# Softmax weights left undivided through the value product, divided afterwards by reciprocals that return from DRAM as rows

## The chip, the cores and the metric

One core of a Trainium2 chip runs one launch of a hybrid decoder layer. The metric is device time of the launch in microseconds (us); lower is better. Engines: TensorE (PE; its weight loads are shown apart, as PEld), VectorE (DVE), ScalarE (ACT), GpSimd (POOL) and SyncE (SP), which issues nearly all DMAs here.

## The reference, cut to what matters

One layer, 512 tokens, 2048 channels. Two of its three token mixers are attentions over heads of 64:

```python
# A: 8 heads, mixture of three dilated causal patterns, combined by their softmax denominators
# C: 16 query heads, 2 kv heads, causal window 128, a learned sink per head
p = jnp.exp(s - m[..., None])
denom = jnp.sum(p, axis=-1)
denom = denom + jnp.exp(sk - m)          # C only: the sink
o = jnp.einsum('nbhgqk,nbkhd->nbqhgd', p, vb)
o = o / denom_t[..., None]
...
x = x + mix @ w_out[l]
```

So the division by the softmax sum comes after the product with v in the reference; it may as well be made on the weights before it. Around the mixers stand the input projection (2048 to 3840 columns), a convolution mixer (B), the output projection, and a SwiGLU block with 5632 hidden channels, all in float32.

## The kernel before

**Stages.** The input projection runs as 30 tiles of 128 columns (PROJ gives their order: cv, ck, then the c queries between b's u and gate tiles, then the a tiles), each 48 matmuls of 128x512: every factor is split in a high and a low part and three products are summed. The output projection follows in two halves, first over eight c row tiles and then over the rest (ROWS), then the up and down products, which take from about 500 us to the end. The change touches only mixers a and c.

**What sets the order.** Every engine runs its instructions in the order in which the program writes them. The program is written along TensorE's projections: `ticks` counts steps of two k tiles (6 matmuls; in the output half later 12), and `ticks.after(n, fn)` puts a piece of a mixer n steps on. C_TICKS and A_TICKS give the distances between a mixer's pieces. Weights come through seven raw buffers, loaded by `pump` (L243, on SP) as soon as the split that read a buffer is done; `split_up_to` makes the high part on ACT (L289, wh) and the low part on DVE (L263, wl), two units ahead of TensorE. 73 slots of 128x512 hold all else.

**A mixer** (`attention`, L795 on, names c0 to c7 and a0 to a3) is a pair of heads; its two halves `head(0)` and `head(1)` fill the two halves of the partitions of one row tile `mix`. Of each head: `scores` (L814, L815, PE), masks and row maxima on DVE, exponentials on ACT (L835 for c, with their sums; L889 for a), then the division on DVE: for c the sink is added, the reciprocal of the four sums of a token is taken (L842), and one product scales all 128x512 weights (L844). For a each of three blocks is multiplied by the mask's counts with its sums (L896), its reciprocal taken (L898), and its one or two row tiles are scaled (L900). PE turns the weights (L850, L916, tiles c1t, a0t and so on), they are split in high (ACT) and low (DVE, c1lp, a0pl), for c sorted to blocks on POOL (L870 and L873, tiles c1ph, c1pl), and `weigh` multiplies them with v (L940 and L941, tiles c1o, a1o). `out_high` (L949, ACT) and `out_rows` (L954, DVE) add the two parts into `mix`. `split_mix` makes mh and ml of a row tile for the output projection (L994, L995), and `residual` (L1073) adds a product to xr.

**Trips through DRAM.** The sums of squares of a q or k tile leave at L642 and come back turned at L647; the scales of a k tile leave at L708 and come back as rows, each broadcast over 64 partitions, at L714, for `scale` on DVE (L723).

Of the kernel before, what the change touches and what calls it, by code (L numbers as in the profile page):

```python
# [9 lines left out]
F32 = mybir.dt.float32  # L10
# [4 lines left out]
ALU = mybir.AluOpType  # L15

P = 128
T = 512
NT = T // P
D = 2048  # L20
KT = D // P
HD = 64
HALF = (slice(0, HD), slice(HD, 2 * HD))
# [93 lines left out]
def kernel(ctx: ExitStack, tc: tile.TileContext, xT, wi, wo, wgu, wd, cst_in, outT):  # L117
    nc = tc.nc
    cp = ctx.enter_context(tc.tile_pool(name="consts", bufs=1))
# [16 lines left out]
    ticks = Ticks()  # L136

    def slot(name, dt=F32, cols=T):
        return sp.tile([P, cols], dt, name=name, tag="s")
# [11 lines left out]
    sums = defaultdict(list)  # L151
# [23 lines left out]
    def up_block(pair, m, half, j):  # L175
# [4 lines left out]
    bufs = {"A": dict(zip(("21", "11", "s", "22"), ("21a", "22a", "sa", "22b"))),  # L180
            "B": dict(zip(("21", "11", "s", "22"), ("21b", "11", "12", "sb")))}

    for n in range(2 * NBLOCKS):
# [15 lines left out]
        bufs = {c: {"21": b["22"], "11": b["21"], "s": b["s"], "22": b["11"]} for c, b in bufs.items()}  # L199
# [6 lines left out]
    for t, (g, r) in enumerate(DOWN):  # L206
# [7 lines left out]
        for k in ("21A", "11A", "21B", "11B", "22A", "22B", "12A", "12B"):  # L214
            c = k[2]
# [14 lines left out]
        bufs = {c: {"21": b["22"], "11": b["21"], "s": b["s"], "22": b["11"]} for c, b in bufs.items()}  # L230
# [255 lines left out]
    for k in range(KT):  # L486
# [9 lines left out]
        elif k < 4 or k % 2 == 0:  # L496
            wh, wl = next_unit()
            o = 0
# [294 lines left out]
    def attention(kind, box, mix, mi, heads):  # L793
# [3 lines left out]
            fl, we = fl + 2, we + 3  # L797
        name = mi
        us = UNITS[kind]
        st = {}  # L800

        def head(h):
            es = {}
            d = cp.tile([P, 4, NT], F32, name=f"{name}d{h}", tag="soft", bufs=6)
            mx, nm, den, rd = (d[:, i] for i in range(4))
            banks = {}

# [32 lines left out]
            def packed_norm():  # L840
                nc.vector.tensor_add(den, den, mx)
                nc.vector.reciprocal(rd, den)  # L842
                by = es["e"].rearrange("p (i c) -> p i c", c=P)
                nc.vector.tensor_mul(by, by, rd[:, :, None].to_broadcast([P, NT, P]))  # L844

            def packed_flip():
                b = bank(f"{name}t{h}")
# [43 lines left out]

            def norm(u):
                e = es[u]
                s = slice(us[u][0][0], us[u][-1][0] + 1)
                for i, k0, n, o in us[u]:
                    nc.vector.scalar_tensor_tensor(e[:, o:o + n], e[:, o:o + n], 1.0, mult_a[:, T - n:],  # L896
                                                   op0=ALU.mult, op1=ALU.mult, accum_out=den[:, i:i + 1])
                nc.vector.reciprocal(rd[:, s], den[:, s])  # L898
                for i, k0, n, o in us[u]:
                    nc.vector.tensor_scalar(e[:, o:o + n], e[:, o:o + n], rd[:, i:i + 1], None, op0=ALU.mult)  # L900

            ph, pl = {}, {}

# [42 lines left out]
            def out_high(b):  # L946
                if h == 0:
                    st["mix"] = slot(f"mix_{mi}")
                nc.scalar.copy(st["mix"][HALF[h]], b[HALF[1 - h]])  # L949
                ticks.after(EV, out_rows, b)  # L950

            def out_rows(b):
                m = st["mix"]
                nc.vector.tensor_add(m[HALF[h]], m[HALF[h]], b[HALF[h]])  # L954
                if h == 1:
                    mix[mi] = m
                    if late:
                        ticks.after(1, split_mix, mi)

            at_v = (len(us) - 1) * step + s1 + sx + s2 + fl + len(TBANKS[kind]) - 1 + ev + EV + we  # L960
            t0 = max(ticks.now + ready, head_at[0], box["q at"] - s1, box["k at"], box["v at"] - at_v)
            head_at[0] = t0 + every
            t0 -= ticks.now
            for u in range(len(us)):
                tu = t0 + u * step
                ticks.after(tu, scores, u)
                if kind == "c":
                    ticks.after(tu + s1, pack, u)
                    continue
                ticks.after(tu + s1, top, u)  # L970
                ticks.after(tu + s1 + sx, exps, u)
                ticks.after(tu + s1 + sx + s2, norm, u)
            tu = t0 + (len(us) - 1) * step + s1 + sx
            if kind == "c":
                ticks.after(tu, packed_exps)
                ticks.after(tu + s2, packed_norm)
                ticks.after(tu + s2 + fl, packed_flip)
            else:
                for t in range(len(TBANKS[kind])):
                    ticks.after(tu + s2 + fl + t, flip, t)  # L980
            ticks.after(t0 + at_v, weigh)

        head(0)
        head(1)


    mix, late = {}, []
# [34 lines left out]
    for name in PROJ[HEAD4:]:  # L1022
        kind, what, j = name[0], name[1], name[2:]
        if name == PROJ[-2]:
            for n, row in enumerate(ROWS[:8]):
                ticks.after(6 + n, split_mix, row)
        b = project(name)
        if kind == "b":
            ticks.after(0, glu_u if what == "u" else glu, int(j), b)
            continue  # L1030
        if kind == "c":
            box = Heads(shared) if j else shared
        else:
            box = boxes.setdefault(j, {})
        if what == "k":
            do_k(box, b, name, 1 if kind == "c" else 0)
        elif what == "v":
            do_v(box, b, name)
        else:
            do_q(box, b, name)  # L1040
        if what == "q":
            if kind == "a":
                boxes.pop(j)
            attention(kind, box, mix, kind + j, (int(j), int(j) + 8) if kind == "c" else None)
# [85 lines left out]
    for half in range(2):  # L1130
        for i, n in enumerate(OUT_ORDER[half]):
# [4 lines left out]
            for kk in range(8):  # L1136
# [4 lines left out]
                s = slice(kk * P, (kk + 1) * P)  # L1141
# [552 lines left out]
```

## Time and profile before

| | us |
|---|---|
| timed runs, median of 3 (lowest, highest) | 1843.22 (1843.0, 1843.69) |
| the profiled execution's own time | 1845.39 |
| its span, first instruction to last | 1843.6 |
| PE busy | 1835.2 |
| DVE busy | 1445.8 |
| ACT busy | 1312.1 |
| POOL busy | 1026.2 |
| TensorE's granted clock | 1.00 of full speed |

Times in a row of the profile count from the span's start. "Idle before, releaser" in a row, and the view of waits, tell what ended an engine's idle time. A window's row gives the busy time of each engine in a stretch and the count of its instructions. Matmuls are pipelined, and their ends in the trace are modelled.

### The profile page before, as it was taken

The page shows a single profiled execution, that of the slowest core. Times are in us where ns is not written, and L with a number is a line of the kernel's source. Part 1 is how long each engine was busy: PE and PEld are TensorE (multiplying, and loading weights), DVE is VectorE, ACT ScalarE, POOL GpSimd, SP SyncE. Part 2 cuts the span into 40 slices and gives each one's busy share as a digit, 9 for nine tenths or more (in the row PEclk, how much of TensorE's full clock was granted, in tenths as well). Part 3 has the DMA queues.
Part 4 walks back from the last instruction along what each step waited for, and adds up shares of the span by engine and source line. Part 5 has one row for each costly group of instructions (what it writes and reads, how often), then busy time and mean ns, then how long its engine had stood idle before and what let it go on. Part 6 is the DMA issues. An engine that isn't in the chain of part 4 may idle for free.

```text
span 1843.6 us, 26502 instructions
## 1 busy us (share of the span) xinstructions
PE 1835.2 (100%) x8314; PEld 1522.4 (83%) x8314; DVE 1445.8 (78%) x2063; ACT 1312.1 (71%) x1784; POOL 1026.2 (56%) x790
## 2 busy tenths in 40 slices
PE   9999999999999999999999999999999999999998
PEld 7888888888888888888888888888888888888887
DVE  6789988997689877778777787777777777777777
ACT  6345554553458788888888888888887778777775
POOL 0126644110003557886788767878676558776552
PEclk9999999999999999999999999999999999999999
DMA  7353345353343457677867778677687679877735
GB/s 276 87 150 93 87 121 153 107 161 116 124 149 103 115 151 191 188 213 182 225 187 200 201 188 226 181 209 199 182 273 258 204 225 295 257 254 260 240 119 110
DMA packets 398924, 334.61 MB, mean 181 GB/s; under 512 B 184256, under 2 KB 326720, under 8 KB 398784
## 3 DMA queue, kind: packets, MB, share of 16 engines
q1 hardware_dynamic: 398208, 332.14, 62.3%
q8 instruction: 66, 1.08, 0.3%
q10 hardware_dynamic: 576, 0.79, 0.1%
q14 instruction: 74, 0.61, 0.1%
HBM read 258.46 MB, written 65.98 MB: 176 GB/s over the span
## 4 chain that ended last, share of the span: by engine, by line
PE 95%; DVE 3%; DMA 1%; issue 0%; ACT 0%; SPq 0%; POOL 0%; DVEq 0%; POOLq 0%; ACTq 0%
PE out L1281 15%; PE out L1279 15%; PE out L1282 15%; PE out L1544 7%; PE out L1546 7%; PE out L1545 7%; PE o L322 3%; PE o L323 3%; PE o L324 3%; PE cq L322 2%; PE cq L324 2%; PE cq L323 2%; PE in L324 1%; PE in L323 1%; PE in L322 1%; PE aq L322 1%
## 5 line engine op out<-in xcount | busy, mean ns | idle before, releaser
L1279 PE MATMUL out<-wh,h 128*128 128x512 f32 x1232 | 479.2, 389 | 0.0
L1281 PE MATMUL out<-wl,h 128*128 128x512 f32 x1232 | 479.2, 389 | 0.0
L1282 PE MATMUL out<-wh,h 128*128 128x512 f32 x1232 | 479.2, 389 | 0.0
L1279 PEld LDWEIGHTS out<-wh,h 128*128 128x128 f32 x1232 | 231.2, 188 | 48.1
L1282 PEld LDWEIGHTS out<-wh,h 128*128 128x128 f32 x1232 | 231.2, 188 | 48.0
L1281 PEld LDWEIGHTS out<-wl,h 128*128 128x128 f32 x1232 | 231.2, 188 | 47.9
L1545 PE MATMUL out<-wl,a 128*128 128x512 f32 x620 | 240.4, 388 | 0.1
L1544 PE MATMUL out<-wh,a 128*128 128x512 f32 x620 | 240.4, 388 | 0.0
L1546 PE MATMUL out<-wh,a 128*128 128x512 f32 x620 | 240.3, 388 | 0.0
L289 ACT CAST wh<-w 128x1024 fp32r<-128x1024 f32 (+2 forms) x94 | 96.9, 1031 | 121.6 <-PE o L323 48.0
L1554 DVE TENSOR_TENSOR y<-y,out 128x512 f32<-128x512 f32 x192 | 128.5, 684 | 47.8 <-PE out L1546 46.1
L263 DVE TENSOR_TENSOR wl<-w,wh 128x1024 fp32r<-128x1024 f32 (+2 forms) x95 | 115.0, 1211 | 30.9 <-ACT wh L289 27.9
L1545 PEld LDWEIGHTS out<-wl,a 128*128 128x128 f32 x620 | 116.4, 188 | 24.5 <-DVE wl L285 0.5
L1546 PEld LDWEIGHTS out<-wh,a 128*128 128x128 f32 x620 | 116.4, 188 | 23.8
L1544 PEld LDWEIGHTS out<-wh,a 128*128 128x128 f32 x620 | 116.4, 188 | 23.8
L573 DVE SCALAR_TENSOR_TENSOR y<-bu,cst,y 128x511 f32<-128x511 f32 (+14 forms) x120 | 92.0, 767 | 1.3
L322 PE MATMUL o<-mh_c,wh 128*128 128x512 f32 x128 | 51.1, 399 | 0.2 <-DVE xr L1073 0.2
L322 PE MATMUL cq<-hh,wh 128*128 128x512 f32 x128 | 50.3, 393 | 0.0
L324 PE MATMUL o<-mh_c,wl 128*128 128x512 f32 x128 | 50.0, 391 | 0.0
L323 PE MATMUL o<-ml_c,wh 128*128 128x512 f32 x128 | 50.0, 390 | 0.0
L323 PE MATMUL cq<-hl,wh 128*128 128x512 f32 x128 | 49.9, 390 | 0.0
L324 PE MATMUL cq<-hh,wl 128*128 128x512 f32 x128 | 49.9, 390 | 0.0
(2351 smaller groups left out, 4766.5 us busy)
## 6 DMA issues: line engine op xcount, KB each, us to landing
od<-a SPq DMA_DIRECT2D x154, 256.0 KB
a<-od SPq DMA_DIRECT2D x154, 256.0 KB
w<-in_wi SPq DMA_DIRECT2D x58, 512.0 KB
w<-in_wo SPq DMA_DIRECT2D x32, 512.0 KB
x<-in_xT SPq DMA_DIRECT2D x16, 256.0 KB
xr<-in_xT SPq DMA_DIRECT2D x16, 256.0 KB
x2d<-xr SPq DMA_DIRECT2D x16, 256.0 KB
z<-x2d SPq DMA_DIRECT2D x64, 64.0 KB
```

What stands on the lines that cost most here:

```text
L263: fn(*args)
L289: (nc.vector.tensor_copy if u == 0 else nc.scalar.copy)(hi[:, :n], t[:, :n])
L322: nc.tensor.matmul(out, wh, xh, start=start, stop=False)
L323: nc.tensor.matmul(out, wh, xl, start=False, stop=False)
L324: nc.tensor.matmul(out, wl, xh, start=False, stop=stop)
L1279: nc.tensor.matmul(b, x[:, high], wh[:, s], start=c == f == 0 and q in (7, 1, 5, 2), stop=False, skip_group_check=True)
L1281: nc.tensor.matmul(b, x[:, high], wl[:, s], start=False, stop=False, skip_group_check=True)
L1282: nc.tensor.matmul(b, x[:, low], wh[:, s], start=False, stop=c == f == 1, skip_group_check=True)
L1544: nc.tensor.matmul(b[:, lo:hi], x[:, high], wh[:, s], start=start, stop=False, skip_group_check=True)
L1545: nc.tensor.matmul(b[:, lo:hi], x[:, high], wl[:, s], start=False, stop=False, skip_group_check=True)
L1546: nc.tensor.matmul(b[:, lo:hi], x[:, low], wh[:, s], start=False, stop=last, skip_group_check=True)
L1554: getattr(eng, op)(t, t, src)
```

## The change

The division moves behind the product with v. The weights e are turned and multiplied as they come from the exponentials (c) or from the masks' counts (a). The reciprocals rd of a head's 512 sums (128 partitions by 4) are written to a DRAM tile `sums`, one word at a time, so that they stand there as a row of 512 (`sums_leave`). Two steps ahead of the second head's product with v, both rows are read back, each broadcast over the 64 partitions of its half (`sums_back`, a new slot `by`). One step after the second half of `mix` is added, one product on DVE multiplies the whole row tile by `by` (`scale_out`), and what followed there (`mix[mi] = m`, `split_mix`) comes after it. For a, one reciprocal is taken of all four columns after the last block, in place of three. The pool of the small tiles d grows from 6 to 8.

```diff
-        st = {}
+        st = {"sums": tc.dram_tile([2, T], F32, name=f"{name}sums")}
+
+        def sums_leave(h, rd):
+            nc.sync.dma_start(st["sums"][h].rearrange("(i p) -> p i", p=P), rd)
+
+        def sums_back():
+            st["by"] = slot(f"{name}by")
+            for h in range(2):
+                nc.sync.dma_start(st["by"][HALF[h]], st["sums"][h:h + 1].to_broadcast([HD, T]))
+
+        def scale_out():
+            m = st["mix"]
+            nc.vector.tensor_mul(m, m, st.pop("by"))
+            mix[mi] = m
+            if late:
+                ticks.after(1, split_mix, mi)
...
-            d = cp.tile([P, 4, NT], F32, name=f"{name}d{h}", tag="soft", bufs=6)
+            d = cp.tile([P, 4, NT], F32, name=f"{name}d{h}", tag="soft", bufs=8)
...
                 nc.vector.reciprocal(rd, den)
-                by = es["e"].rearrange("p (i c) -> p i c", c=P)
-                nc.vector.tensor_mul(by, by, rd[:, :, None].to_broadcast([P, NT, P]))
+                ticks.after(1, sums_leave, h, rd)
...
-                nc.vector.reciprocal(rd[:, s], den[:, s])
-                for i, k0, n, o in us[u]:
-                    nc.vector.tensor_scalar(e[:, o:o + n], e[:, o:o + n], rd[:, i:i + 1], None, op0=ALU.mult)
+                if u == len(us) - 1:
+                    nc.vector.reciprocal(rd, den)
+                    ticks.after(1, sums_leave, h, rd)
...
                 if h == 1:
-                    mix[mi] = m
-                    if late:
-                        ticks.after(1, split_mix, mi)
+                    ticks.after(1, scale_out)
...
             ticks.after(t0 + at_v, weigh)
+            if h == 1:
+                ticks.after(t0 + at_v - 2, sums_back)
```

The order of PE and of POOL is the same in both kernels; ACT's differs in one or two places by a row. Three places on DVE and SP follow (out<-in by the program's names with buffer numbers; the changed kernel's lines are 13 to 15 higher).

DVE at about 173 to 178 us of the profile before, in the second head of c1, ahead of the gate tile bg that ACT and POOL wait for. Before:

```order
L573 SCALAR_TENSOR_TENSOR y_1218<-bu_708,cst,y_1218 128x491
L841 TENSOR_TENSOR c1d_1131<-c1d_1131 128x4
L842 RECIPROCAL c1d_1131<-c1d_1131 128x4
L844 TENSOR_TENSOR c1e_1701<-c1e_1701,c1d_1131 128x512
L562 TENSOR_TENSOR bg_1765<-bg_1585,r1b 128x512
L263 TENSOR_TENSOR wl_1742<-w_1288,wh_1741 128x1024
```

Now:

```order
L573 SCALAR_TENSOR_TENSOR y_1221<-bu_708,cst,y_1221 128x491
L856 TENSOR_TENSOR c1d_1134<-c1d_1134 128x4
L857 RECIPROCAL c1d_1134<-c1d_1134 128x4
L562 TENSOR_TENSOR bg_1776<-bg_1594,r1b 128x512
L263 TENSOR_TENSOR wl_1754<-w_1291,wh_1753 128x1024
```

The scaling of the weights between the reciprocal and bg is gone.

SP at about 150 to 177 us before, with the loads of raw weights (w) and the trip of cq2. Before:

```order
L243 DMA w_1602<-in_wi 128x1024
L642 DMA cq2d<-cq2p 32x4x4 x4
L685 DMA cq_1580<-cq2l 64x512
L686 DMA cq_1581<-cq2l 64x512
L243 DMA w_1697<-in_wi 128x1024
L647 DMA cq2t<-cq2d 128x16
L243 DMA w_1775<-in_wi 128x1024
L243 DMA w_1843<-in_wi 128x1024
```

Now:

```order
L243 DMA w_1611<-in_wi 128x1024
L803 DMA c1sums<-c1d_1133 128x4x1
L642 DMA cq2d<-cq2p 32x4x4 x4
L685 DMA cq_1588<-cq2l 64x512
L686 DMA cq_1589<-cq2l 64x512
L243 DMA w_1706<-in_wi 128x1024
L647 DMA cq2t<-cq2d 128x16
L808 DMA c3by<-c3sums 64x512 x2
L243 DMA w_1786<-in_wi 128x1024
L803 DMA c1sums<-c1d_1134 128x4x1
L243 DMA w_1856<-in_wi 128x1024
```

A write of c1's first sums comes ahead of the trip of cq2, the two reads of c3's rows behind it, and a write of c1's second sums between two loads.

DVE at about 396 to 403 us before, at the start of the output projection, where a1's row tile is finished and the residual xr of an output tile follows. Before:

```order
L954 TENSOR_TENSOR mix_a_4081<-mix_a_4081,a1o_4199 64x512
L995 TENSOR_TENSOR ml_a_4268<-mix_a_4081,mh_a_4267 128x512
L263 TENSOR_TENSOR wl_4191<-w_3735,wh_4190 128x1024
L896 SCALAR_TENSOR_TENSOR a2e_4253,a2d_3860<-a2e_4253,mult_a 128x512
L898 RECIPROCAL a2d_3860<-a2d_3860 128x1
L900 TENSOR_SCALAR a2e_4253<-a2e_4253,a2d_3860 128x512
L880 ISA a2s_4255,a2d_3861<-a2s_4255,bias_a 128x256
L880 ISA a2d_3861 128x1
L880 ISA a2s_4255,a2d_3861<-a2s_4255,bias_a 128x128
L880 ISA a2d_3861 128x1
L883 SCALAR_TENSOR_TENSOR a2d_3861<-a2d_3861,aq2r 128x2
L1073 TENSOR_TENSOR xr_4183<-xr_4183,o_0_4187 128x512
```

Now:

```order
L967 TENSOR_TENSOR mix_a_4108<-mix_a_4108,a1o_4230 64x512
L812 TENSOR_TENSOR mix_a_4108<-mix_a_4108,a1by 128x512
L263 TENSOR_TENSOR wl_4222<-w_3764,wh_4221 128x1024
L909 SCALAR_TENSOR_TENSOR a2e_4279,a2d_3891<-a2e_4279,mult_a 128x512
L912 RECIPROCAL a2d_3891<-a2d_3891 128x4
L894 ISA a2s_4281,a2d_3892<-a2s_4281,bias_a 128x256
L894 ISA a2d_3892 128x1
L894 ISA a2s_4281,a2d_3892<-a2s_4281,bias_a 128x128
L894 ISA a2d_3892 128x1
L897 SCALAR_TENSOR_TENSOR a2d_3892<-a2d_3892,aq2r 128x2
L1008 TENSOR_TENSOR ml_a_4315<-mix_a_4108,mh_a_4314 128x512
L1086 TENSOR_TENSOR xr_4214<-xr_4214,o_0_4218 128x512
```

The product with the rows (a1by) stands where the low part ml_a stood; ml_a now comes right ahead of xr, and the scaling of a2's last block is gone.

More of the change, by code (lines that the diff above doesn't have):

```diff
@@ L893, in norm @@
                 e = es[u]
-                s = slice(us[u][0][0], us[u][-1][0] + 1)
                 for i, k0, n, o in us[u]:
```

## Prediction

> **What bounds the kernel now.** I read the page first: the span, the busy shares and the shares of the chain that ended last.
>
> ```profile
> span 1843.6 us, 26502 instructions
> PE 1835.2 (100%) x8314; PEld 1522.4 (83%) x8314; DVE 1445.8 (78%) x2063; ACT 1312.1 (71%) x1784; POOL 1026.2 (56%) x790
> ...
> PE 95%; DVE 3%; DMA 1%; issue 0%; ACT 0%; SPq 0%; POOL 0%; DVEq 0%; POOLq 0%; ACTq 0%
> ```
>
> PE is idle for 1843.6 - 1835.2 = 8.4 us in all. The change lies in the projections and the first half of the output product, about 110 to 500 us, so I cut that stretch into windows (columns: PE, PEld, DVE, ACT, POOL busy, each with its count, then clock, DMA share, GB/s), with one quiet window from the later stage beside it.
>
> ```profile
> 175.00:200.00 25.00, 24.19 (x125) 20.20 (x124) 24.09 (x46) 13.90 (x32) 16.61 (x24) 1.00 0.26 75
> 325.00:350.00 25.00, 24.72 (x129) 20.80 (x128) 23.34 (x62) 11.45 (x19) 5.06 (x11) 1.00 0.32 84
> 350.00:375.00 25.00, 24.83 (x123) 20.53 (x121) 24.35 (x68) 12.34 (x22) 2.67 (x2) 1.00 0.34 94
> 650.00:675.00 25.00, 25.00 (x112) 20.70 (x111) 20.09 (x24) 21.11 (x24) 19.57 (x10) 1.00 0.62 171
> ```
>
> The reader should see two things. DVE is nearly full here (24.1 and 24.4 of 25 us), and still PE loses only a few tenths per window: 0.81, 0.28 and 0.17 us. So taking work from DVE pays only where PE visibly waits. Those places are the next view, the waits of PE between 100 and 500 us (total, times, longest), and under it those of its weight loads.
>
> ```profile
> PE c1o L941 <- POOL c1pl L873: 0.8, 2, 0.5
> PE a0t L916 <- DVE a0e L900: 0.3, 1, 0.3
> PE o L322 <- DVE xr L1073: 0.2, 1, 0.2
> PE a1t L916 <- DVE a1e L900: 0.2, 1, 0.2
> ```
>
> ```profile
> PEld c1o L941 <- POOL c1pl L873: 1.3, 2, 0.8
> ...
> PEld o L322 <- ACT a2e L889: 0.6, 1, 0.6
> PEld a0t L916 <- DVE a0e L900: 0.5, 1, 0.5
> PEld a1t L916 <- DVE a1e L900: 0.4, 1, 0.4
> ```
>
> Four places, 0.8 + 0.3 + 0.2 + 0.2 = 1.5 us by PE's rows and 1.3 + 0.6 + 0.5 + 0.4 = 2.8 us by the loads'. Matmul ends are modelled, so a gap may be partly hidden under the matmul drawn before it, and I take the loss to lie between. That is all that this stage has to give.
>
> The weight loads' 83% is weighed against that. The quiet window has 20.70 of 25 us, also 83%, at 112 matmuls and with PE busy throughout, so 83% is what a stretch without waits looks like here. The Trainium skill (Perfetto Trace Analysis, section "Identifying the Most-Contended Engine") says to judge TensorE's headroom by the share of LDWEIGHTS and by the useful arithmetic, not by matmul busy time; by that rule 17% is free and DVE could be the bound. The quiet window speaks against it; its time is rival 3.
>
> **The change part by part: DVE.** These rows are the operations taken out, with the ns of one (c kind; two of the four groups of the a kind; its reciprocals).
>
> ```profile
> L844 DVE TENSOR_TENSOR c1e<-c1e,c1d x2: 691/692/692, 164.2 to 174.2; 128x512 f32<-128x512 f32 x2
> ```
>
> ```profile
> L900 DVE TENSOR_SCALAR a0e<-a0e,a0d 128x128 f32<-128x128 f32 (+3 forms) x8 | 3.0, 392 | 0.2
> ...
> L900 DVE TENSOR_SCALAR a2e<-a2e,a2d 128x128 f32<-128x128 f32 (+3 forms) x8 | 2.9, 384 | 0.2
> ```
>
> ```profile
> L898 DVE RECIPROCAL a0d<-a0d x6: 164/164/167, 320.4 to 345.3; 128x1 f32<-128x1 f32 x4, 128x2 f32<-128x2 f32 x2
> ```
>
> The eight c mixers lose 16 x 0.692 = 11.1 us; the four a mixers lose 3.0 + 3 x 2.9 = 11.7 us of scalings and, with 24 reciprocals becoming 8, 16 x 0.164 = 2.6 us. Added are 12 products of a row tile with its reciprocals, 128x512 with two inputs in SBUF. That is the form of L844, so 0.692 each; the bounds are the a kind's longest scaling, 0.485, below, and about double a L844 above. 12 x 0.692 = 8.3 us. DVE sheds 11.1 + 11.7 + 2.6 - 8.3 = 17.1 us (8.8 to 19.6 with those bounds for the product).
>
> What lies on the path is only what ends PE's four waits. The first one hangs on a chain through three engines:
>
> ```profile
> 174.21 0.69 DVE L844 TENSOR_TENSOR c1e<-c1e,c1d 128x512 f32<-128x512 f32 x1
> 174.82 0.68 DVE L562 TENSOR_TENSOR bg<-bg,r1b 128x512 f32<-128x512 f32 x1
> ...
> 175.54 0.63 ACT L563 ACTIVATE bg<-bg 128x512 f32<-128x512 f32 x1 [2.01 <-DVE bg L562]
> ...
> 176.25 1.53 POOL L564 TENSOR_TENSOR bu<-bu,bg 128x512 f32<-128x512 f32 x1 [3.41 <-ACT bg L563]
> ```
>
> ACT waited 2.01 us for DVE's bg, POOL 3.41 us for ACT, and POOL's queue behind it (the powers of cq2, then the selections of c1's weights) ends in the wait of c1o. DVE runs back to back here (no idle in brackets), and in the new order the scaling ahead of bg is gone, here and in the row above that began at 164.2, so bg comes at least 2 x 0.69 = 1.4 us sooner (c3's product is queued only after it). POOL moves up with it, by more than the longest single wait of 0.8 us: both waits of c1o should go. The waits of a0t and a1t are for the last scaling of a weight block; that scaling is gone, and the turn needs only the mask product, a reciprocal (0.16) and a scaling (0.485) earlier: both go. The fourth is in this view, DVE, and last the matmul that waited:
>
> ```profile
> 396.52 0.69 DVE L954 TENSOR_TENSOR mix_a<-mix_a,a1o 64x512 f32<-64x512 f32 x1 [0.47 <-ACT mix_a L949]
> 397.90 0.69 DVE L995 TENSOR_TENSOR ml_a<-mix_a,mh_a 128x512 fp32r<-128x512 f32 x1 [0.69 <-ACT mh_a L994]
> ...
> 400.57 0.48 DVE L900 TENSOR_SCALAR a2e<-a2e,a2d 128x512 f32<-128x512 f32 x1
> ...
> 402.21 0.69 DVE L1073 TENSOR_TENSOR xr<-xr,o 128x512 f32<-128x512 f32 x1
> ...
> 403.05 0.47 PE L322 MATMUL o<-mh_c,wh 128*128 128x512 f32 x1 [0.20 <-DVE xr L1073]
> ```
>
> Here a1's product comes in (+0.69), the idle 0.69 before ml_a goes because ml_a is queued later, and the scaling goes (-0.48): xr ends about 0.5 us sooner, and the wait goes too. Of 1.5 to 2.8 us I take **2.2**, the middle.
>
> **The change part by part: SP and the DMAs.** New are 24 writes of 512 words of 4 bytes and 12 pairs of broadcast reads. The k scales already make such a trip; these are its rows in the view of one tile, then the page's line of the queue, then two of SP's waits.
>
> ```profile
> L708 SPq DMA_DIRECT2D cke<-ckwide x4: 289/294/432, 92.7 to 93.9; - x4
> L714 SPq DMA_DIRECT2D ckwide<-cke x2: 477/532/588, 95.3 to 95.8; - x2
> ...
> L723 DVE SCALAR_TENSOR_TENSOR ckk<-ckraw,gqk,ckwide x1: 753/753/753, 99.3 to 99.3; 128x512 f32<-128x512 f32 x1
> ```
>
> ```profile
> q1 hardware_dynamic: 398208, 332.14, 62.3%
> ```
>
> ```profile
> SPq L243 <- DVE wl L263: 143.7, 38, 9.2
> ...
> SPq L647 <- DMA ak1d<-ak1p: 2.2, 1, 2.2
> ```
>
> A write and its receipt took 95.3 - 93.9 = 1.4 us and, by the wait of L647, up to 2.2 us; the pair of reads, of the very shape that is added, was issued from 95.3 to 96.4, and DVE used it at 99.3 without a wait, so it landed within 2.9 us. SP spends 24 x 0.43 + 12 x 1.1 = 23.5 us more on issuing over some 340 us. That hides in what SP waits anyway: 143.7 us, 38 times, for a split to free a weight buffer, seven raw buffers ahead of PE. For the queue no row has 4-byte writes: from nothing up to the mean of all packets, 62.3% of 16 x 1843.6 us over 398208 = 46 ns, hence 12288 x 46 ns / 16 = 35 us spread over 340, where the windows' DMA share is 0.26 to 0.34. I take nothing, being nearer the light end: the head sums' writes at L642, in pieces of four words, were back within the 2.2 us that L647 waited.
>
> The added wait is DVE's, in the product, and behind it stand the weight splits wl and the residual xr that PE needs. From the order, SP issues c3's pair behind cq2t (169.3 us) and DVE multiplies after 181.6; the tightest is a1: issued behind a weight load and used after mix_a:
>
> ```profile
> 389.89 0.45 SPq L243 DMA_DIRECT2D w<-in_wo x1
> ```
>
> So a1's pair is issued at about 390.4 to 391.5, lands by 394.4, and is wanted at 397.2: 2.8 us to spare. **Sum**: no cost, 2.2 us gained. The profiled execution took 1845.39 us, its span 1843.6 and 1.8 around it; it would become 1843.2. The three timed runs have a median of 1843.22, 2.2 below it, so I forecast 1841.0.
>
> **The rivals.** (1) *Nothing is gained*: the waits of c1o end with POOL's own queue, whose selections are uneven, and the three others with the next instruction on DVE. Against it: each wait names an operation that is removed or moves up. 1843.2.
> (2) *Slower: the reciprocals come late.* Mechanism: a write of 512 single words takes far longer than one in pieces of four words, or SP is held up ahead of the reads; DVE, in order, stands in the product of a1, and xr behind it holds PE's next output tile. It decides once a1's pair lands after about 397.7 (397.2 and the 0.5 us won). With 12 us from issue instead of 2.9 it would land at 402.4, PE would wait 4.7 us there, and the next tightest, c4 and a0, I estimate at 2 us together: 1841.0 + 7 = 1848. For it speaks that 4-byte writes are not in the trace; against it the trips of the k scales and head sums.
> (3) *DVE is the bound of this stage*, and its 17.1 us pass through: 1843.2 - 17.1 = 1826. For it DVE's 24 of 25 us; against it PE's count of matmuls in those windows.
> (4) *The short delays go as well.* First matmuls of a unit are slower here than in the later stage:
>
> ```profile
> L322 PE MATMUL aq<-hh,wh 128*128 128x512 f32 x64 | 25.8, 403 | 0.0
> ...
> L322 PE MATMUL o<-mh_c,wh 128*128 128x512 f32 x128 | 51.1, 399 | 0.2 <-DVE xr L1073 0.2
> ```
>
> Against 389, 64 x 14 ns + 128 x 10 ns = 2.2 us; were that DVE's doing, 1841.0 - 2.2 = 1838.8, and with the like of other projections 1837.
>
> **How the numbers follow.** Forecast 0.71 (1839.7 to 1842.4, by the bounds 1.5 and 2.8 and some reading error), nothing gained 0.12 (up to 1844.5 with a little new waiting), late reciprocals 0.12, DVE the bound 0.02, short delays 0.03. The range 1839.7 to 1844.6 holds the first two, 0.83. 0.2% is 3.7 us, about what a measurement of this kernel can tell from no change: faster takes rivals 3 and 4, 0.05; slower rival 2, 0.12; within it the rest, 0.83.
>
> **What would show it.** Right: the waits of PE on c1pl, a0e, a1e and xr are gone or under 0.1 us each, DVE's busy time is about 17 us lower with more idle before wl, and no row in which DVE waits for a DMA of the by tiles. Wrong: such a row followed by a wait of PE for wl or xr; new waits on POOL; or a span shorter by far more than PE's old waits, with fewer ns per matmul.

## The result, and the profile after

The changed kernel takes 1897.47 us (median of 5 runs, 1896.72 to 1898.2), against 1843.69 (1843.0 to 1845.19) for the kernel before: ratio 1.0291, 95% interval 1.0277 to 1.0304. The prediction was 1841.0 and its range ended at 1844.6. It was wrong: about 54 us were lost where 2.2 were to be won. The profiled execution took 1897.93 us, its span 1896.1.

From the page of the changed kernel: the span, the busy shares, and the DMA queue of the loads and trips.

```profile
span 1896.1 us, 26530 instructions
PE 1853.6 (98%) x8314; PEld 1532.8 (81%) x8314; DVE 1429.6 (75%) x2011; ACT 1312.7 (69%) x1784; POOL 1009.9 (53%) x790
...
q1 hardware_dynamic: 412800, 335.33, 66.2%
```

DVE shed 1445.8 - 1429.6 = 16.2 us, nearly as forecast. PE is now idle for 1896.1 - 1853.6 = 42.5 us, 34.1 more than before, and the same 8314 matmuls are drawn 18.4 us longer. The two make the 52.5 us by which the span grew. On the queue, 0.662 x 1896.1 = 1255 us were busy against 0.623 x 1843.6 = 1149: 106 us more of all 16 engines, for 24 writes that move 2 KB each and 12 pairs of reads (which alone bring 12 us, by run 3 below: 0.625 x 1842.2 against 0.619 x 1841.2).

The windows of the changed kernel, in the columns of the prediction's:

```profile
125.00:150.00 25.00, 20.82 (x97) 17.11 (x96) 18.93 (x43) 10.55 (x28) 8.78 (x19) 0.88 0.70 70
175.00:200.00 25.00, 19.94 (x93) 16.04 (x92) 23.13 (x47) 11.32 (x27) 14.72 (x21) 0.90 0.57 86
275.00:300.00 25.00, 20.71 (x97) 16.84 (x96) 17.39 (x36) 9.13 (x26) 3.41 (x4) 1.00 0.73 119
300.00:325.00 25.00, 19.55 (x83) 15.67 (x84) 17.91 (x31) 9.99 (x16) 11.55 (x20) 0.80 0.73 145
325.00:350.00 25.00, 23.21 (x110) 18.91 (x109) 16.46 (x35) 9.69 (x27) 6.58 (x10) 1.00 0.55 117
350.00:375.00 25.00, 17.98 (x68) 14.62 (x69) 17.54 (x39) 9.85 (x18) 8.48 (x14) 0.81 0.55 139
650.00:675.00 25.00, 25.00 (x112) 20.71 (x111) 22.47 (x30) 20.46 (x23) 12.10 (x6) 1.00 0.50 121
```

Three columns matter. In the windows at 175, 325 and 350 PE has 93, 110 and 68 matmuls where it had 125, 129 and 123; the late window is untouched. The granted clock fell to between 0.80 and 0.90 in four windows. And from 175 to 200 the DMA share rose from 0.26 to 0.57 while the rate went only from 75 to 86 GB/s: the DMA engines are not moving more, their packets take longer.

The eight largest waits of PE in the changed kernel (total, times, longest):

```profile
PE c6o L954 <- POOL c6pl L887: 7.3, 3, 3.4
PE c4o L953 <- POOL c4ph L887: 7.0, 1, 7.0
PE o L322 <- DVE xr L1086: 3.9, 1, 3.9
PE c0o L953 <- POOL c0ph L887: 3.4, 1, 3.4
PE c4o L954 <- POOL c4pl L887: 2.6, 3, 1.6
PE c1o L953 <- POOL c1ph L887: 2.0, 1, 2.0
PE c6o L953 <- POOL c6ph L887: 1.5, 2, 1.1
PE a1t L929 <- DVE a1e L909: 1.5, 1, 1.5
```

Six of the eight name POOL's selections, which the change does not touch, and POOL is busy for less time than before. So the next question is what POOL waits for. Take the first case. SP of the changed kernel, from c0's first write to the second:

```profile
123.09 0.37 SPq L803 DMA_DIRECT2D c0sums<-c0d  x1
123.73 1.74 SPq L642 DMA_DIRECT2D cq1d<-cq1p  x4
125.57 0.47 SPq L685 DMA_DIRECT2D cq<-cq1l  x1
126.08 0.59 SPq L686 DMA_DIRECT2D cq<-cq1l  x1
126.72 0.58 SPq L243 DMA_DIRECT2D w<-in_wi  x1
136.97 0.34 SPq L647 DMA_DIRECT2D cq1t<-cq1d  x1
```

The sums of squares of cq1 leave behind the write and come back only after 136.97, since SP waited 8.9 us for their receipt. The same trip in the kernel before:

```profile
125.63 1.74 SPq L642 DMA_DIRECT2D cq1d<-cq1p  x4
...
129.39 0.34 SPq L647 DMA_DIRECT2D cq1t<-cq1d  x1
```

There the way back was issued 2.0 us after the way out, and 11.5 us after it in the changed kernel. From here the delay goes on through POOL and PE of the changed kernel:

```profile
139.57 0.74 POOL L655 TENSOR_TENSOR cq1r<-cq1t 128x8 f32<-128x8 f32 x1 [20.90 <-DMA cq1t<-cq1d]
...
142.63 0.41 POOL L884 TENSOR_SCALAR_AFFINE_SELECT c0ph<-c0hp 128x256 fp32r<-128x256 f32 x1
142.99 0.94 POOL L887 TENSOR_SCALAR_AFFINE_SELECT c0ph<-c0hp 128x256 fp32r<-128x256 f32 x1
```

```profile
143.99 0.58 PE L953 MATMUL c0o<-c0ph,cv 128*128 128x256 f32 x1 [3.44 <-POOL c0ph L887]
```

The first of these rows, POOL's for cq1, in the kernel before:

```profile
132.62 0.60 POOL L655 TENSOR_TENSOR cq1r<-cq1t 128x8 f32<-128x8 f32 x1 [12.74 <-DMA cq1t<-cq1d]
```

POOL runs in order. It stood 20.90 us before the first power of cq1, where it stood 12.74 before, and c0's selections, queued behind, came 3.44 us too late for PE. The DMA engines of the changed kernel between 122 and 140 us, in 40 slices (busy tenths, then GB/s), and below them those of the kernel before:

```profile
DMA  0000421110588990000988000504995946410029
GB/s 0 0 0 0 4 5 4 4 4 2 132 191 200 178 27 0 0 0 0 27 18 18 0 0 0 27 9 36 73 73 64 155 118 255 182 17 1 0 82 264
```

```profile
DMA  0000000000111129996998798310100000000011
GB/s 0 0 0 0 0 0 0 0 0 2 4 4 5 5 73 205 214 200 155 364 400 214 232 337 328 137 73 0 36 0 0 0 0 0 0 0 0 0 5 5
```

Before, the stretch of loads ran through, mostly at 150 to 400 GB/s. Now it starts, and from about 128.7 to 133.5 us hardly anything moves. The 512 words themselves seem done within about 1 us in the packets' records; it is what stands behind them that halts. SP then waits for receipts all over the stage. Three of its longest waits for a trip of q, k or v in the changed kernel, and the trip of ak0, which the runs below follow (before, the longest single wait for such a trip between 100 and 500 us was 2.2):

```profile
SPq L759 <- DMA av2d<-av2t: 12.8, 1, 12.8
...
SPq L647 <- DMA cq1d<-cq1p: 9.5, 2, 8.9
...
SPq L647 <- DMA cq2d<-cq2p: 7.4, 3, 6.8
SPq L714 <- DMA ak0e<-ak0wide: 7.4, 1, 7.4
```

DVE did wait for the rows too, as the prediction feared, but not at a1:

```profile
DVE mix_c L812 <- DMA c0by<-c0sums: 7.3, 1, 7.3
...
DVE mix_a L812 <- DMA a0by<-a0sums: 3.8, 1, 3.8
DVE mix_c L812 <- DMA c4by<-c4sums: 2.3, 1, 2.3
```

### The profile page after: what moved, and what is told of

Read it like the earlier page. It is cut to its first block, busy times and chain, and to the rows that moved or that the text cites. A ratio compares the mean times of both kernels' runs of the same rounds, so it can differ in the third digit from the quotient of the medians.

```text
span 1896.1 us, 26530 instructions
## 1 busy us (share of the span) xinstructions
PE 1853.6 (98%) x8314; PEld 1532.8 (81%) x8314; DVE 1429.6 (75%) x2011; ACT 1312.7 (69%) x1784; POOL 1009.9 (53%) x790
## 4 chain that ended last, share of the span: by engine, by line
PE 71%; DVE 1%; DMA 0%; issue 0%; ACT 0%; DVEq 0%; SPq 0%
PE out L1294 15%; PE out L1295 15%; PE out L1292 15%; PE out L1557 7%; PE out L1559 7%; PE out L1558 7%; PE o L323 2%; PE o L324 2%; PE o L322 2%; DVE y L1567 0%; DVE wl L285 0%; DMA out_T<-z 0%; DVE z L1466 0%; DVE lnv L412 0%; DVE y L1536 0%
```

## The experiments

**Theory A**: each write of 512 single words halts the DMAs behind it for some 8 us; trips of q, k and v come late, POOL and PE with them. **Rivals**: B, DVE stands in its products until the rows are there, and holds up the rest; C, the broadcast reads, or SP's issuing of them, get in the way; D, the new order on DVE (the product, the single reciprocal of a) is worse than the old one. Unless said otherwise an edit is made to the changed kernel. All but the turned and the packed version leave the division out or use rows that are not the sums' (the product on DVE stays, by the rows r1b that lie in SBUF). The kernel before ran on the same chip each time; ratios are to it. Diffs are cut to the lines that matter.

**1. No trip at all.**

```diff
-            nc.sync.dma_start(st["sums"][h].rearrange("(i p) -> p i", p=P), rd)
+            pass
...
-            st["by"] = slot(f"{name}by")
-            for h in range(2):
-                nc.sync.dma_start(st["by"][HALF[h]], st["sums"][h:h + 1].to_broadcast([HD, T]))
+            pass
...
-            nc.vector.tensor_mul(m, m, st.pop("by"))
+            nc.vector.tensor_mul(m, m, r1b)
```

> The changed kernel without any trip: neither the writes of the sums nor the reads, and the row tile is multiplied by a row tile that lies in SBUF anyway (norm 1's scales), so this part of the result is left out. What the change does to DVE's order stays. Theory A (each write of 512 single words holds up all DMAs behind it for some 8 to 9 us, and the q, k and v trips that stand behind it come late): 1841 to 1843 us, PE's old waits of 1.5 us gone or nearly. Theory B (DVE, standing in the product for the rows that come back, is what costs): the same here. Theory C (the broadcast reads of one DRAM row cost): the same. Theory D (the new order on DVE or the undivided weights themselves cost): above 1880.

Measured 1843.77 us, 0.9999 (0.9991 to 1.0008). The whole loss is gone, with DVE's new order in place: D falls.

**2. The writes alone** (the second and third edit above, with the writes left in).

> The changed kernel with the 24 writes of the sums but without the reads; the product takes norm 1's scales, so the division itself is left out, and DVE waits for no rows. Theory A: 1885 to 1898, since the writes alone hold up the other trips; the wait of the cq1 trip for its write's receipt (8.9 us in the changed kernel, about 2 before) stays. Theory B: 1841 to 1846. Theory C: 1841 to 1846.

Measured 1884.88 us (1880.18 to 1891.09), 1.0234 (1.0217 to 1.0251): about 43 of the 54 us, with nobody reading the rows and nobody waiting for them. So A carries most of it. SP's and PE's longest waits in this run:

```profile
SPq L647 <- DMA cq1d<-cq1p: 9.1, 1, 9.1
...
SPq L714 <- DMA ak0e<-ak0wide: 8.4, 2, 8.2
```

```profile
PE c6s L827 <- DMA cq<-cq6l: 9.7, 1, 9.7
PE c6o L952 <- POOL c6pl L885: 5.9, 3, 2.8
```

Here PE waited 9.7 us even for a q tile itself (cq6), which SP moves by DMA.

Where the queue's time went is told by the records of single packets in the traces of runs 1 and 2. Run 2 has 106 us more of all 16 engines. Packets of 4 bytes make 8 us of it, at 9 ns each on average; packets of 4096 bytes, of which the loads of raw weights in this stage consist (11520 in both runs), make 89. In run 1 none of these took over 1.3 us. In run 2 312 of them took over 2 us, the longest 9.5. Each of the 312 started within 14 us of the issue of a write, and 20 of the 24 writes have some behind them. So the single words are not slow by their own records: the loads that come behind them are.

**3. The reads alone**, of two rows stored early.

```diff
         def sums_leave(h, rd):
-            nc.sync.dma_start(st["sums"][h].rearrange("(i p) -> p i", p=P), rd)
+            pass
...
-                nc.sync.dma_start(st["by"][HALF[h]], st["sums"][h:h + 1].to_broadcast([HD, T]))
+                nc.sync.dma_start(st["by"][HALF[h]], rows2[h:h + 1].to_broadcast([HD, T]))
```

> The changed kernel with the 12 pairs of broadcast reads, but of two rows that are written once, early and as rows of 2 KB; the 24 writes are left out, and so is the division proper. DVE still waits for the rows. Theory A: 1841 to 1844, rows landing within 3 us and no row of DVE waiting for them. Theory B: the same if the rows come in time, 1845 to 1855 if the reads are slow by themselves. Theory C: 1885 to 1898.

Measured 1843.12 us, 0.9993 (0.9984 to 1.0002), and no row in which DVE waits for a by tile. C falls: 12 pairs of reads, SP's time for them and 12 products cost nothing by themselves.

**4. The whole change, the reciprocals turned on DVE** so that they leave in pieces of 128 bytes: one more 128x32 transpose per mixer, and 4 writes instead of 2, which leave once both heads are done. Cut from the diff: a small tile w with a memset on POOL, and the DRAM tile and the reads in the layout of the pieces.

```diff
+                nc.vector.transpose(w[:, 32:64], w[:, :32])
...
-            nc.sync.dma_start(st["sums"][h].rearrange("(i p) -> p i", p=P), rd)
+            for a in range(4):
+                nc.sync.dma_start(st["sums"][:, 32 * a:32 * a + 32], w[32 * a:32 * a + 2 * NT, 32:64])
```

> The whole change, but the reciprocals of both heads are turned on DVE first (one transpose of 128x32 for each mixer, as the k scales do it) and leave as four writes of 8 rows of 128 bytes, 32 pieces in all for each mixer in place of 1024 of 4 bytes. Theory A: 1841 to 1845, so below or level with the kernel before. Theory B and C: 1880 to 1898, since the product's wait and the reads are the same.

Measured 1843.48 us, 0.9996 (0.9987 to 1.0005). The same data takes the same way, and the loss is gone. Two of its windows, and all that the view of PE's waits between 100 and 500 us has:

```profile
125.00:150.00 25.00, 25.00 (x132) 21.23 (x131) 24.30 (x52) 14.49 (x39) 17.05 (x23) 1.00 0.47 139
...
350.00:375.00 25.00, 25.00 (x128) 21.16 (x127) 23.23 (x54) 14.41 (x24) 3.86 (x5) 1.00 0.43 120
```

```profile
PE lv L472 <- DVE lnv L412: 0.5, 1, 0.5
```

So the writes of single words it is, and B is at most the rest. What about them is slow? The next runs keep the writes only (like run 2) and change their shape.

**5. Pieces of 16 bytes**, as many as before, side by side over 8 KB: each partition sends all 16 words of its small tile d, to a DRAM tile of 512 rows of 4 words for each head.

```diff
-            nc.sync.dma_start(st["sums"][h].rearrange("(i p) -> p i", p=P), rd)
+            nc.sync.dma_start(st["sums"][h].rearrange("(j p) f -> p j f", p=P), d)
```

> This run leaves the division out, as the run with the 24 writes alone did; each write still has 512 pieces, but pieces of 16 bytes instead of 4, so 8 KB one after another in DRAM. If the cost lies in the pieces being single words (size), it falls to the kernel before's time, 1843 to 1846. If it lies in the number of pieces of one write (count), it stays at 1880 to 1890, and SP waits 6 to 9 us for a trip's write in several places. If it lies in neighbouring pieces sharing a short stretch of DRAM (place), four pieces in 64 bytes instead of sixteen, I expect something between, 1850 to 1865.

Measured 1844.04 us, 1.0003 (0.9993 to 1.0012). The number of pieces is not it. My middle value for *place* was wrong as well.

**6 and 7. Single words, 64 bytes apart and 512 bytes apart** (n is 16 or 128 words).

```diff
-        st = {"sums": tc.dram_tile([2, T], F32, name=f"{name}sums")}
+        st = {"sums": [tc.dram_tile([T, n], F32, name=f"{name}sums{h}") for h in range(2)]}
...
-            nc.sync.dma_start(st["sums"][h].rearrange("(i p) -> p i", p=P), rd)
+            nc.sync.dma_start(st["sums"][h].rearrange("(i p) f -> p i f", p=P)[:, :, 0], rd)
```

> Division left out, 24 writes of 512 single words, each word 64 bytes from the next in DRAM. Size or count: no change against the writes alone, 1880 to 1890. Place, with lines of 64 bytes as what is shared: 1843 to 1846; with a longer stretch as what is shared (512 bytes, say): still about 1880.

> Division left out, 24 writes of 512 single words, each word 512 bytes from the next in DRAM. Size or count: 1880 to 1890 as before. Place, whatever stretch up to 512 bytes is shared: 1843 to 1846.

Measured 1843.12 us, 1.0000 (0.9990 to 1.0009), and 1843.39, 1.0000 (0.9991 to 1.0010). Words of 4 bytes, 512 to a write, cost nothing once they lie 64 bytes apart: neither their size nor their number. In run 6 no packet of a load took over 1.4 us. The same trip of the k scales as in run 2, at 64 bytes:

```profile
SPq L714 <- DMA ak0e<-ak0wide: 1.2, 2, 1.0
```

**8. A quarter of the words**, still side by side.

```diff
-            nc.sync.dma_start(st["sums"][h].rearrange("(i p) -> p i", p=P), rd)
+            nc.sync.dma_start(st["sums"][h, :P].rearrange("(i p) -> p i", p=P), rd[:, :1])
```

> Division left out, 24 writes of only 128 single words (one column of four). If each word costs a share of the 8 to 9 us for which other transfers stand still, a write holds them up about 2.2 us: most waits of SP for a trip's receipt fall below 4 us, and the time is 1843 to 1850. If the hold-up is a fixed price of such a write, it stays near 1880.

Measured 1868.94 us, 1.0141 (1.0125 to 1.0156): 26 us, over half the cost with a quarter of the words, so neither a share for each word nor, in time, one fixed price. On the queue it is nearly one: 93 us against 106 (table below). Words packed as densely still stall, with the same trip in between:

```profile
SPq L714 <- DMA ak0e<-ak0wide: 6.2, 2, 5.6
```

**9. The whole change in another order of words**: a partition's four reciprocals leave as one piece of 16 bytes, in the same 2 KB, and the product reads the row with a stride.

```diff
-            nc.sync.dma_start(st["sums"][h].rearrange("(i p) -> p i", p=P), rd)
+            nc.sync.dma_start(st["sums"][h].rearrange("(p i) -> p i", i=NT), rd)
...
-            nc.vector.tensor_mul(m, m, st.pop("by"))
+            by = st.pop("by").rearrange("q (p i) -> q i p", i=NT)
+            m3 = m.rearrange("q (i p) -> q i p", p=P)
+            nc.vector.tensor_mul(m3, m3, by)
```

> The whole change, with the words of a row in another order: each partition's four reciprocals leave as one piece of 16 bytes, 128 pieces side by side in the same 2 KB, and the product reads the row with a stride of four words. If single words that share a line of 64 bytes are what stalls the transfers, pieces of 16 bytes, four to a line, cost little or nothing (the write with 512 pieces of 16 bytes cost nothing): 1841 to 1846, and no row of DVE waiting for a by tile. If what counts were the 2 KB that all pieces share, it would lie like the quarter of the words, at about 1865 to 1870. The product with a stride may take longer than the 0.69 us of the plain one; that I expect to be hidden.

Measured 1842.8 us, 0.9998 (0.9989 to 1.0007). Run 8 puts 128 single words into 512 bytes and loses 26 us; here 128 pieces of four words fill 2 KB and lose nothing in time. The loads are not quite untouched: 31 of their packets took over 2 us, the longest 2.5. The pieces of runs 5 and 9 also start 16 bytes apart, so these two runs do not tell the size of a piece from its distance to the next; the next run does.

**10. Single words 16 bytes apart**, as in run 6 with n = 4.

> Division left out, 24 writes of 512 single words, each word 16 bytes from the next, so four words to a line of 64 bytes; number, size and places are those of the writes with pieces of 16 bytes, except that three quarters of each place are not written. If pieces that fill their place escape the cost, and single words pay for every neighbour in a line, the time lies between the words side by side (1885) and the words 64 bytes apart (1843): by a quarter of the cost at 16 to a line, 1850 to 1856. If only the number of neighbours in a line counts and four are few, 1843 to 1846, as with 16 bytes.

Measured 1845.21 us, 1.0008 (0.9999 to 1.0018): 0 to 3 us, less than the proportional share that I expected. So single words at the distance of run 5's pieces cost little or nothing too: it is the distance.

**11. Single words 8 bytes apart**, n = 2.

> Division left out, 24 writes of 512 single words, each word 8 bytes from the next, so eight to a line of 64 bytes. Sixteen to a line cost 41 us, four to a line at most 3, one to a line nothing. If the hold-up grows with the number of words that share a line, it lies between: at half the hold-up of about 8 us, 4 us behind each write, as the quarter of the words had, 1855 to 1870. If it is neighbours of one full 64-byte line being written in every word that cost (as with 16 to a line alone), it is 1843 to 1848.

Measured 1850.65 us, 1.0033 (1.0021 to 1.0046). Between, as the theory has it, but below the 1855 to 1870 that I gave for it. The runs together; "queue time" is the share of q1 times the span, less the same of run 1 (1139.7 us), and the last column is SP's longest wait for the trip of ak0:

| writes of 512 words | ratio | queue time, us | ak0 trip, us |
|---|---|---|---|
| 512 B or 64 B apart | 1.0000 | +9, +13 | 1.1, 1.0 |
| 16 B apart | 1.0008 | +17 | 2.3 |
| 8 B apart | 1.0033 | +27 | 4.0 |
| side by side | 1.0234 | +106 | 8.2 |
| side by side, 128 words | 1.0141 | +93 | 5.6 |

The kernel before, with the same packets as run 1, differs from it by 9 us of queue time too, so the +9 and +13 are hardly more than nothing. From there the hold-up grows with how closely the words are packed, and the time follows late. That the trips have a couple of us to spare would fit; it was not measured apart.

**12. All writes, and reads of two early rows**: what is the rest from run 2 to the change?

```diff
-                nc.sync.dma_start(st["by"][HALF[h]], st["sums"][h:h + 1].to_broadcast([HD, T]))
+                nc.sync.dma_start(st["by"][HALF[h]], rows2[h:h + 1].to_broadcast([HD, T]))
```

> All 24 writes of the change, and its 12 pairs of reads and products, but the rows read are two that were stored long before, so that no read has to wait for a write's receipt; the values of the division are therefore not the reference's. The change costs 1897, its writes alone 1885. If the 12 us between are DVE's products standing for the late rows, and the rows are late because SP must wait for the write's receipt before it issues the read, it falls to 1885 to 1889. If the reads are late because they queue behind stalled transfers, whosever rows they are, it stays at 1893 to 1898, with rows of DVE waiting for the by tiles.

Measured 1890.66 us (1884.77 to 1895.5), 1.0254 (1.0235 to 1.0272), between the two, and not clear of run 2. DVE waits although nothing has to come back first (the profiled execution is the longest of the four, 1895.5):

```profile
DVE mix_c L813 <- DMA c0by<-rows: 5.4, 1, 5.4
DVE mix_a L813 <- DMA a0by<-rows: 4.8, 1, 4.8
DVE mix_c L813 <- DMA c2by<-rows: 2.3, 1, 2.3
```

So reads do stand behind stalled transfers, whosever rows they are. How the last 12 us divide between that and the wait for the write's receipt is not settled: the intervals are as wide as the parts.

## Why the prediction was wrong, point by point

**The step that failed** is the cost of the writes on the queue: "I take nothing, being nearer the light end: the head sums' writes at L642, in pieces of four words, were back within the 2.2 us that L647 waited." Run 9 shows that this row was right about pieces of four words; it says nothing about single words side by side, which no row had. The sum priced the words' own packets, 0 to 35 us, and these did take only about 8. But the queue lost 106 us in run 2, 89 of them in the packets of the loads behind the words, so the upper bound was too low. And spread over 340 us it was weighed as occupancy, where there is room. It came as halts of what stands behind, up to 9.5 us for one packet of a load, and SP's waits for receipts grew to as much as 12.8 us. A bound by the time of its own packets does not cover what a transfer does to others.

**Rival 2 (late reciprocals)** had the right trigger, "a write of 512 single words takes far longer", with the wrong victim: it followed only the rows themselves to DVE and xr, priced 7 us. The rows' own lateness is within the 12 us or so between run 2 and the change. I listed what stands behind the waiting instruction on DVE, but not what stands behind the writes on the DMA queues: the trips of q, k and v. The order shown with the change has the sums of cq2 right behind a write, ahead of the rows.

**The tightest place** was named as a1, with 2.8 us to spare. In the stalled kernel c0 (7.3), a0 (3.8), c4 (2.3) and c3 (1.1) waited and a1 did not. In runs 4 and 9 no by tile was waited for, which fits the landing times that were forecast for an open queue.

**PE's four waits** go, as forecast: in runs 4 and 9 the only wait left there is lv's 0.5 us. But that one is new: the kernel before has none for lv (in run 1 c6o also waits 1.0 us for POOL). PE's idle time in all went only from 8.4 us to 1840.2 - 1832.4 = 7.8 in run 4 and 1840.5 - 1832.4 = 8.1 in run 9. So this term of the sum was probably too large as well: what was taken from the four places came back in part at others. In time, run 4 gives -0.7 us (-2.4 to +0.9, by 1843.5 times its interval) and run 9 -0.4 (-2.0 to +1.3): of the 2.2 us nothing is confirmed, and up to 2.4 are possible. So without the halts the result would be told best by **rival 1** (nothing gained): by its time, and in part by its mechanism, since the four waits are gone but others took their place.

**DVE** shed 16.2 us against 17.1. **Rival 3** (DVE as the bound) falls by run 4: DVE lost about as much work, 1427.9 us busy, and the time did not move. The weight loads' 81% in the changed kernel goes with a PE that is idle 2%: here their share fell as PE's waits grew. **SP's issuing** cost nothing, by run 3 for the reads and run 4 for its own 48 writes.

**Rival 4** (shorter first matmuls) falls by the same two groups of matmuls in run 4, which have the 399 and 403 ns of before to the last digit:

```profile
L322 PE MATMUL o<-mh_c,wh 128*128 128x512 f32 x128 | 51.0, 399 | 0.0
...
L322 PE MATMUL aq<-hh,wh 128*128 128x512 f32 x64 | 25.8, 403 | 0.0
```

**The clock** was not in the prediction. Its 18.4 us are a consequence of PE's waits. Take the window at 300, with 0.80: PE stood from 295.7 to 302.7 us for c4's selections. In windows of 2.5 us the granted clock is still 1.00 to 300, 0.66 in the next, 0.50 from 302.5 to 310, and 1.00 again from 312.5. A stretch ahead of the wait and one behind it, PE busy throughout in both, with 13 matmuls and with 8:

```profile
290.00:292.50 2.50, 2.50 (x13) 2.07 (x12) 2.20 (x5) 0.43 (x1) 0.00 (x0) 1.00 0.50 107
307.50:310.00 2.50, 2.50 (x8) 2.02 (x8) 2.46 (x4) 1.99 (x3) 2.27 (x4) 0.50 0.14 5
```

The Trainium skill (TensorE: Matmul & The Clock Gate, section "What's actually happening") has the array at half clock after an idle window of about 3.4 us. The trace agrees: here the clock fell after some 5 us of idle. So each long wait of PE is paid a second time.

## What to carry to other kernels

Where a change adds a kind of transfer that the trace has no row of, price it by what is queued behind it, not by its share of the queue, and let the range reach to a halt of that queue. A column of words that must become a row in DRAM should leave in pieces of 16 bytes or more (turn it first, or let the reader take the stride), or with its words 64 bytes apart: these are the shapes that cost nothing here. And when PE waits for an engine whose work did not change, ask what that engine waits for until a DMA's receipt turns up.

## What the runs showed of the hardware

Single words written side by side by one DMA held up the DMAs behind them: in run 2 SP waited up to 9.1 us for a receipt and a single packet of a load took up to 9.5, although the words' own packets are recorded as short (9 ns on average). By the trip of ak0, which takes 1.0 us at 64 bytes apart, the hold-up was about 7 us side by side, 3 at 8 bytes and 1 at 16. The Trainium skill (DMA: Bandwidth & Descriptors, section "Specifications") says that transfers below 512 bytes are done as read-modify-write. That alone does not give this: the words 64 and 512 bytes apart are as short and cost nothing. That neighbouring words wait for each other in the memory would fit, but it is only argued: the runs show spacing, and not how long a stretch is shared, nor where the transfers stand.

The strided product of run 9 took 1.03 to 1.31 us where the plain one takes 0.69; its first row:

```profile
L814 DVE TENSOR_TENSOR mix_c<-mix_c,c0by x1: 1155/1155/1155, 154.4 to 154.4; 128x512 f32<-128x512 f32 x1
```

DVE's busy time rose only to 1432.4 us from run 4's 1427.9, and it was hidden.
